# Row vectors that are put in order by two ScalarE copies

## The chip, the cores and the metric

One core of a Trainium2 chip runs the whole program. The time is in microseconds (us) of the device, from the start of the program to its end; three runs of a kernel are given by their median. The engines are named as the profile names them: PE (TensorE matmul; PEld is its weight load), DVE (VectorE), ACT (ScalarE), POOL (GpSimd) and SP (SyncE, which issues the DMAs).

## The reference, cut to what matters

Three transformer layers on 512 tokens of width 1024, in float32. Each sublayer is wrapped in the same two formulas; a third one closes the kernel:

```python
def rms_norm(x, g):
    y = x * rsqrt(mean(x * x, axis=-1) + 1e-6)
    return y * g

mod = silu(c) @ ada_w[layer] + ada_b[layer]            # six vectors of 1024
sh1, sc1, g1, sh2, sc2, g2 = split(mod, 6)
h = rms_norm(x, norm_g[0]) * (1 + sc1) + sh1           # into the sublayer
x = x + g1 * rms_norm(y, norm_g[1])                    # behind it
...
return x + gate * out                                  # last layer
```

So at every border between two sublayers each row of `x` is multiplied elementwise by vectors of 1024 that are the same for every row: `G` (gate times norm gain), `B` (one plus scale, times norm gain) and `S` (shift). In the last layer it is `gate`.

## The kernel before

Everything is recorded as a list of operations first (`Rec.add`), with a cost for each from a formula (`Rec.cost`: for a DVE operation 68 + 1.043 ns per element, for an ACT copy from SBUF 93 + 0.834 ns per element, both whatever the operands' steps). Then a list scheduler (`Rec.order`, `Rec.once`) replays the list on a model of the engines. It picks for each engine the most urgent operation that is ready, gives every tile a slot in a pool of fixed size, and repeats this 12 times with due times worked out from the last pass (`dates`). Of the passes the one with the earliest modelled end is kept. Then each engine gets its operations in that order (`emit`); on the chip every engine follows its own list, and waits where an operand is not there yet. Tiles of up to 2 KB per partition share pool "2", which has 12 slots. A tile may take a slot only while enough are free for all the tiles that come before it in the program and have none yet (`Res.rank`, `place`). A DMA is modelled as landing 650 + 1350 ns and its transfer time (256 KB: 790 ns) after its issue (lines 549 to 551).

A weight GEMM is done in three passes of float32r (high part, and two corrections), so PE has most of the work, and DVE and ACT (now and then POOL) split weights and activations into high and low parts (`wh`, `wl`, `ah`, `al`, in the tail of a GEMM `twh`, `twl`, `tah`, `tal`).

A row vector is first computed with a feature on each partition, a column tile of 128 x 8 (`col`). `wide` (line 953) brings it onto all 128 partitions: one DMA writes the 1024 values to DRAM so that four values of one partition lie side by side, two DMAs read 512 of them each onto all partitions. Thus in the tile the value of feature `128 k + p` of a half stands at `4 p + k`. `wide` returns the tile through a rearranged view, whose innermost step is four elements (16 bytes); the instructions that use it get their other operands through `by4` (line 964), which only names the two axes.

Eleven vectors go through `wide`: `G1, B2, S2` at the end of the first mixer (`gmlp`), `G2` after the first feed-forward layer (its `B` and `S` stay columns, `h_chunk2`), `G3, B4, S4` after the attention (`nsa`), `G5, B6, S6` after the second feed-forward layer, and `gate` at the end of `second`. In the profile the tiles are called `G1w`, `B2w` and so on, and `gatew`. Their users are these:

- `residual` (line 1032), four borders, four chunks of 128 rows, two halves: `z = acc * G` (DVE reads the accumulators in PSUM), then `x = x + r * z`.
- `h_chunk` (line 1002), three borders: `hx = x * B` and then `hx = hx * r + S`, both on DVE or POOL as the scheduler likes; then four PE transposes of `hx` into `tp`, and the split of `tp` into the next layer's `hi` and `lo`.
- `fin` (line 1987): `fy = acc * gate`, then `fy + fx` and the DMA of the result.

`three(rows)` (line 1126) makes the wide tiles; `gmlp` and `nsa` call it ahead of the whole output GEMM, `ff` at `k == 31 - FTAIL`, so eight weight blocks before its end. In `out_gemm` the last `tail` blocks of the contraction are held in SBUF, and the chunks are finished one after the other, so that `done(c, banks)` of a chunk runs while PE does the next chunk.

Of the kernel before, what the change touches and what calls it, by code (L numbers as in the profile page):

```python
# [26 lines left out]
F32 = mybir.dt.float32  # L27
# [645 lines left out]
class KB:  # L673
# [279 lines left out]
    def wide(self, vec, name):  # L953

        v = self.col(vec)
        r = self.scratch([1, 1024], name)
        self.sp.dma_start(r.rearrange("o (n p k) -> p (o n) k", n=2, p=128), v.rearrange("p (n k) -> p n k", n=2))
        t = [self.t2([128, 512], F32, name) for _ in range(2)]
        for n in range(2):
            self.sp.dma_start(t[n], r[:, n * 512:n * 512 + 512].bcast())  # L960
        return [x.rearrange("q (p k) -> q k p", k=4) for x in t]

    @staticmethod
    def by4(x):

        return x.rearrange("q (k p) -> q k p", k=4)


    def x_rstd(self, c, either=False):
# [32 lines left out]
    def h_chunk(self, c, r, B, S, hT, keep=None):  # L1002
        if keep is not None:
            return self.h_chunk2(c, r, B, S, hT, keep)
        for n in range(2):
            s = slice(n * 512, n * 512 + 512)
            t = self.t2([128, 512], F32, "hx")
            self.flex("tensor_mul", self.by4(t), self.by4(self.xs[c][:, s]), B[n])
            self.mac(self.by4(t), self.by4(t), r, S[n])
            ps = self.ps("tp")  # L1010
            for j in range(4):
                self.pe.transpose(ps[:, j * 128:(j + 1) * 128], t[:, j * 128:(j + 1) * 128], self.ident)
            cs = slice(c * 128, c * 128 + 128)
            self.split(hT.hi[n][:, :, cs], hT.lo[n][:, :, cs], ps.rearrange("p (j t) -> p j t", j=4))
# [17 lines left out]
    def residual(self, c, banks, G):  # L1032

        ss = self.st(2, "ys")
        z = []
        for n in range(2):
            s = slice(n * 512, n * 512 + 512)
            junk = self.t2([128, 512], F32, "junk")
            self.act.activation(junk, banks[n], AF.Square, accum_out=ss[:, n:n + 1])
            z.append(self.t2([128, 512], F32, "z"))  # L1040
            self.dve.tensor_mul(self.by4(z[n]), self.by4(banks[n]), G[n])
        r = self.rstd_of(ss, "yr")
        for n in range(2):
            s = slice(n * 512, n * 512 + 512)
            x = self.xs[c][:, s]
            self.mac(x, z[n], r, x)
# [639 lines left out]
    def second(self, hT, grow):  # L1686
# [298 lines left out]
        gate = self.wide(grow, "gatew")  # L1985

        def fin(c, banks):
            for n in range(2):
                s = slice(n * 512, n * 512 + 512)
                xt = self.t2([128, 512], F32, "fx")  # L1990
                self.sp.dma_start(xt, self.xd[c][:, s])
                y = self.t2([128, 512], F32, "fy")
                parts = 2 if c == NC - 1 and n == 1 else 1
                for i in range(parts):
                    h = slice(i * 512 // parts, (i + 1) * 512 // parts)
                    hk = slice(h.start // 128, h.stop // 128)
                    self.dve.tensor_mul(self.by4(y)[:, hk], self.by4(banks[n])[:, hk], gate[n][:, hk])
                    self.dve.tensor_add(y[:, h], y[:, h], xt[:, h])
                    self.sp.dma_start(self.out[0, c * 128:(c + 1) * 128, n * 512 + h.start:n * 512 + h.stop], y[:, h])

        self.out_gemm(self.act_f32(mixed), I["w_out_2"][0], KD, fin, CTAIL, split=True)

    def build(self):
# [87 lines left out]
```

## Time and profile before

| | |
|---|---|
| median of 3 runs | 1549.9 us (1549.61 to 1550.47) |
| the profiled execution | 1551.63 us, its span 1549.6 us |
| PE busy | 1499.1 us (97% of the span) |
| DVE busy | 1128.3 us (73%) |
| ACT busy | 673.0 us (43%) |
| POOL busy | 246.0 us (16%) |

A busy share is an average over the whole span. The span is that of the profiled execution; what a sum from the trace says of it is carried to the median of the runs, which is 1.7 us below the profiled execution's own time. An instruction's name in the profile is `out<-in`. Nearly all instructions carry line 616, that of the recorder, so tiles tell them apart, not lines.

### The profile page before, as it was taken

What the parts mean: (1) busy time and instruction counts of PE and PEld (TensorE: products, weight loads), DVE (VectorE), ACT (ScalarE), POOL (GpSimd) and SP (SyncE); (2) the same over time, 40 slices, a digit from 0 to 9 for tenths busy, and PEclk for the clock granted to TensorE, in tenths of its full rate; (3) what the DMA queues carried; (4) which work ended last, traced back from release to release, by engine and by line L of the source; (5) the groups of instructions that cost most, each with busy time, mean ns of one, the idle gap of its engine ahead of it and who ended that gap; (6) DMA issues with size and microseconds to landing.
All of it is one profiled execution on the core that took longest, in us unless ns stands there. A gap on an engine that the chain in (4) does not pass through costs nothing.

```text
span 1549.6 us, 20206 instructions
## 1 busy us (share of the span) xinstructions
PE 1499.1 (97%) x7426; PEld 1250.1 (81%) x7426; DVE 1128.3 (73%) x2092; ACT 673.0 (43%) x1466; POOL 246.0 (16%) x286
## 2 busy tenths in 40 slices
PE   8998899999999999999999899999999899999988
PEld 6887788888888888778877788888888778878877
DVE  8898975568871779788996964455671778698983
ACT  6533332232120646688893332221120327567770
POOL 1142000000010311343431000000010005122350
PEclk9999999999999999999999999999999999999999
DMA  9863675549620443101014636337311351113112
GB/s 368 278 231 115 220 272 188 169 156 383 268 86 11 138 145 118 51 1 56 29 69 137 206 121 202 112 135 278 129 55 41 102 173 55 55 55 106 31 55 95
DMA packets 117921, 212.96 MB, mean 137 GB/s; under 512 B 16064, under 2 KB 76736, under 8 KB 117824
## 3 DMA queue, kind: packets, MB, share of 16 engines
q1 hardware_dynamic: 117824, 211.69, 39.8%
q8 instruction: 58, 0.95, 0.2%
q14 instruction: 39, 0.32, 0.1%
HBM read 205.33 MB, written 6.34 MB: 137 GB/s over the span
## 4 chain that ended last, share of the span: by engine, by line
PE 70%; DVE 15%; ACT 3%; issue 2%; POOL 1%; POOLq 0%; DVEq 0%; ACTq 0%
PE acc L616 25%; PE fmps L616 24%; PE qps L616 4%; PE tmc L616 3%; DVE hx L616 3%; PE po L616 2%; PE sgps L616 2%; DVE wl L616 2%; DVE ptl L616 2%; DVE z L616 1%; PE kps L616 1%; DVE x L616 1%; PE sB L616 1%; PE vps L616 1%; PE tmb L616 1%
## 5 line engine op out<-in xcount | busy, mean ns | idle before, releaser
L616 DVE TENSOR_TENSOR wl<-raw,wh 128x1024 fp32r<-128x1024 f32 x194 | 240.7, 1243 | 39.4 <-PE fmps L616 18.5
L616 DVE CAST wh<-raw 128x1024 fp32r<-128x1024 f32 x120 | 84.9, 707 | 133.6 <-PE fmps L616 102.0
L616 PE MATMUL acc<-wh,ah 128*128 128x512 f32 x432 | 168.4, 390 | 0.0
L616 PE MATMUL acc<-wl,ah 128*128 128x512 f32 x432 | 168.3, 390 | 0.0
L616 DVE SCALAR_TENSOR_TENSOR raw<-raw,cb 128x1024 f32<-128x1024 f32 x112 | 136.5, 1244 | 0.0
L616 PE MATMUL acc<-wh,al 128*128 128x512 f32 x432 | 133.3, 389 | 0.0
L616 ACT ACTIVATE r<-fmps 128x512 f32<-128x512 f32 x64 | 38.2, 597 | 205.9 <-PE fmps L616 205.9
L616 PE MATMUL fmps<-hfh,wl 128*128 128x512 f32 (+1 forms) x288 | 105.9, 368 | 1.9 <-DVE wl L616 1.9
L616 PE MATMUL acc<-twh,tah 128*128 128x512 f32 x272 | 106.4, 396 | 0.0
L616 PE MATMUL fmps<-hf1h,wl 128*128 128x512 f32 (+1 forms) x288 | 105.4, 366 | 0.8 <-DVE wl L616 0.8
L616 PE MATMUL acc<-twl,tah 128*128 128x512 f32 x272 | 105.8, 395 | 0.0
L616 PE MATMUL fmps<-hfl,wh 128*128 128x512 f32 (+1 forms) x288 | 105.7, 368 | 0.0
L616 PE MATMUL fmps<-hfh,wh 128*128 128x512 f32 (+1 forms) x288 | 105.5, 368 | 0.0
L616 PE MATMUL fmps<-hf1l,wh 128*128 128x512 f32 (+1 forms) x288 | 105.3, 366 | 0.0
L616 PE MATMUL fmps<-hf1h,wh 128*128 128x512 f32 (+1 forms) x288 | 104.9, 366 | 0.0
L616 ACT CAST ah<-hid 128x512 fp32r<-128x512 f32 x48 | 29.8, 620 | 158.9 <-PE acc L616 158.9
L616 PEld LDWEIGHTS acc<-wh,al 128*128 128x128 f32 x432 | 81.1, 188 | 16.8
L616 PEld LDWEIGHTS acc<-wh,ah 128*128 128x128 f32 x432 | 81.2, 188 | 16.7
L616 PEld LDWEIGHTS acc<-wl,ah 128*128 128x128 f32 x432 | 81.1, 188 | 16.6
L616 PE MATMUL acc<-twh,tal 128*128 128x512 f32 x272 | 87.8, 398 | 4.6 <-DVE tal L616 4.6
L616 POOL TENSOR_SCALAR tah<-hid 128x512 fp32r<-128x512 f32 x4 | 3.9, 969 | 476.3 <-DMA raw<-in_ff_w_out_dram 206.3
L616 ACT CAST wh<-raw 128x1024 fp32r<-128x1024 f32 x55 | 57.6, 1049 | 43.0 <-PE fmps L616 30.0
(533 smaller groups left out, 3869.9 us busy)
## 6 DMA issues: line engine op xcount, KB each, us to landing
raw<-in_ada_w_dram SPq DMA_DIRECT2D x40, 1024.0 KB, 7.5
raw<-in_ff_w_in_dram SPq DMA_DIRECT2D x32, 1024.0 KB, 8.8
raw<-in_ff_w_out_dram SPq DMA_DIRECT2D x32, 1024.0 KB, 5.0
raw<-in_w_in_dram SPq DMA_DIRECT2D x16, 1024.0 KB, 5.5
raw<-in_w_ada_dram SPq DMA_DIRECT2D x12, 1024.0 KB, 6.4
raw<-in_ada_w_dram SPq DMA_DIRECT2D x16, 512.0 KB, 9.9
raw<-in_kv_ada_w_dram SPq DMA_DIRECT2D x8, 1024.0 KB, 12.1
raw<-in_a_w_in_dram SPq DMA_DIRECT2D x8, 512.0 KB, 10.2
```

The costliest lines, as they stand in the source:

```text
L616: getattr(real[e], m)(*a, **k)
```

## The change

`wide` allocates two tiles for each half. The DMA reads into the first (`G1wr` and so on, after its name), an ACT copy puts it in order into the second, and the second is returned as it is. `by4` goes; all users read and write plain contiguous tiles. Nothing else is touched: the DMAs, the arithmetic and the scheduler stay.

```diff
@@ wide
-        t = [self.t2([128, 512], F32, name) for _ in range(2)]
+        t = []
         for n in range(2):
-            self.sp.dma_start(t[n], r[:, n * 512:n * 512 + 512].bcast())
-        return [x.rearrange("q (p k) -> q k p", k=4) for x in t]
-
-    @staticmethod
-    def by4(x):
-
-        return x.rearrange("q (k p) -> q k p", k=4)
+            w = self.t2([128, 512], F32, name + "r")
+            self.sp.dma_start(w, r[:, n * 512:n * 512 + 512].bcast())
+            t.append(self.t2([128, 512], F32, name))
+            self.act.copy(t[n].rearrange("q (k p) -> q k p", k=4), w.rearrange("q (p k) -> q k p", k=4))
+        return t
@@ h_chunk
-            self.flex("tensor_mul", self.by4(t), self.by4(self.xs[c][:, s]), B[n])
-            self.mac(self.by4(t), self.by4(t), r, S[n])
+            self.flex("tensor_mul", t, self.xs[c][:, s], B[n])
+            self.mac(t, t, r, S[n])
@@ residual
-            self.dve.tensor_mul(self.by4(z[n]), self.by4(banks[n]), G[n])
+            self.dve.tensor_mul(z[n], banks[n], G[n])
@@ fin
-                    hk = slice(h.start // 128, h.stop // 128)
-                    self.dve.tensor_mul(self.by4(y)[:, hk], self.by4(banks[n])[:, hk], gate[n][:, hk])
+                    self.dve.tensor_mul(y[:, h], banks[n][:, h], gate[n][:, h])
```

## Rows read from the trace of the kernel before

**Rows 1.** The page's first part: busy time of each engine, share, instructions

```profile
PE 1499.1 (97%) x7426; PEld 1250.1 (81%) x7426; DVE 1128.3 (73%) x2092; ACT 673.0 (43%) x1466; POOL 246.0 (16%) x286
```

**Rows 2.** PE's waits, whole span: waiter, releaser, us in total, times, longest

```profile
PE tp L616 <- DVE hx L616: 14.3, 22, 1.7
...
PE acc L616 <- DVE tal L616: 4.6, 2, 3.1
```

**Rows 3.** Groups by form, DVE, vector users: count, busy us, mean ns, idle before

```profile
L616 DVE SCALAR_TENSOR_TENSOR hx<-hx,xr,S2w 128x512 f32<-128x512 f32 x8 | 8.8, 1142 | 0.2
...
L616 DVE TENSOR_TENSOR z<-acc,G3w 128x512 f32<-128x512 f32 x8 | 8.3, 1072 | 11.6 <-PE acc L616 11.6
...
L616 DVE TENSOR_TENSOR hx<-x,B2w 128x512 f32<-128x512 f32 x7 | 7.3, 1084 | 0.0
L616 DVE TENSOR_TENSOR fy<-acc,gatew 128x512 f32<-128x512 f32 x7 | 7.1, 1056 | 21.9 <-PE acc L616 21.9
```

**Rows 4.** Groups by form, DVE: same operations and sizes on other operands

```profile
L616 DVE TENSOR_TENSOR ptl<-tA,pth 128x512 fp32r<-128x512 f32 x36 | 24.7, 687 | 5.8 <-ACT pth L616 5.4
...
L616 DVE SCALAR_TENSOR_TENSOR x<-z,yr,x 128x512 f32<-128x512 f32 x32 | 22.6, 748 | 0.5
...
L616 DVE TENSOR_TENSOR fy<-fy,fx 128x512 f32<-128x512 f32 x7 | 4.6, 691 | 0.0
```

**Rows 5.** PE's waits at the first mixer's border, 140 to 215 us

```profile
PE tp L616 <- DVE hx L616: 2.1, 4, 1.0
PE fmps L616 <- DVE wl L616: 1.9, 1, 1.9
PE tp L616 <- ACT junk L616: 0.7, 1, 0.7
```

**Rows 6.** PE's waits at the attention's border, 835 to 915 us

```profile
PE tp L616 <- DVE hx L616: 5.4, 8, 1.4
PE fmps L616 <- DVE wl L616: 0.8, 1, 0.8
```

**Rows 7.** PE's waits at the second feed-forward layer's border, 1190 to 1270 us

```profile
PE tp L616 <- DVE hx L616: 5.2, 8, 1.7
```

**Rows 8.** PE's waits at the first feed-forward layer's border, 495 to 560 us

```profile
PE tp L616 <- ACT hx L616: 0.6, 1, 0.6
```

**Rows 9.** Timeline, 1242 to 1252 us: start, length, engine, instruction, idle before

```profile
1242.81 1.05 DVE L616 TENSOR_TENSOR z<-acc,G5w 128x512 f32<-128x512 f32 x1
...
1246.75 2.07 DVE L616 TENSOR_TENSOR hx<-x,B6w 128x512 f32<-128x512 f32 x2
...
1246.87 1.06 ACT L616 ACTIVATE junkx<-x 128x1024 f32<-128x1024 f32 x1 [2.47 <-DVE x L616]
...
1248.74 0.15 DVE L616 TENSOR_SCALAR hv<-ss 128x1 f32<-128x1 f32 x1
...
1250.40 2.18 DVE L616 SCALAR_TENSOR_TENSOR hx<-hx,xr,S6w 128x512 f32<-128x512 f32 x2
1251.67 0.63 PE L616 MATMUL tp<-ident,hx 128*128 128x128 f32 x4 [0.99 <-DVE hx L616]
```

**Rows 10.** Busy us of PE, PEld, DVE, ACT, POOL by stretch, PE clock, DMA

```profile
192.00:194.00 2.00, 2.00 (x11) 2.00 (x11) 1.86 (x4) 0.00 (x0) 0.00 (x0) 0.50 1.00 384
194.00:196.00 2.00, 2.00 (x15) 2.00 (x14) 2.00 (x4) 0.80 (x2) 0.00 (x0) 0.71 1.09 350
800.00:825.00 25.00, 21.81 (x123) 15.77 (x122) 24.48 (x66) 22.12 (x59) 9.46 (x14) 1.00 0.34 105
```

**Rows 11.** DMAs of tile `B4w`: time from issue to landing

```profile
DMA to landing us min/median/max: 2.8/5.6/6.0
```

**Rows 12.** Groups by form, ACT: a plain 512-element pass, one with steps of 64 bytes

```profile
L616 ACT ACTIVATE hid<-r 128x512 f32<-128x512 f32 x64 | 40.5, 633 | 2.0
...
L616 ACT ACTIVATE bh<-R,pos 128x124 fp32r<-128x124 f32 x32 | 14.3, 504 | 4.2 <-DVE R L616 4.2
```

**Rows 13.** Timeline, ACT, 820 to 830 us: first split for the attention's output GEMM

```profile
824.77 0.60 ACT L616 CAST ah<-oT 128x512 fp32r<-128x512 f32 x1
```

## The prediction

> **What bounds the kernel now.** I read the shares of the engines first. PE is busy for 1499.1 of 1549.6 us [rows 1], so about 50 us at most can be won without taking work from PE, and a cheaper DVE instruction is worth something only where PE stands still for it. So the second view is the list of PE's waits. Its longest entry is the transposes `tp` that wait for DVE's `hx`: 14.3 us in 22 waits [rows 2]. `hx` is made by the instructions that the change touches. The third view is the same list cut to the four borders. It shows 2.1 + 0.7 + 1.9 us at the first mixer's border [rows 5], 5.4 + 0.8 us at the attention's [rows 6] and 5.2 us at the second feed-forward layer's [rows 7]. (The 0.7 put down to ACT's `junk` is a `tp` like the others; DVE's `hx` ended last there.) At the first feed-forward layer's border there is a wait of 0.6 us for an ACT `hx`, and none for DVE [rows 8]: that border uses only `G2w`, and the change has nothing to win there.
>
> Why DVE is late is in the groups by form. The users of the wide tiles take 1072 ns (`z`), 1084 ns (`hx` product), 1142 ns (`hx` with the shift) and 1056 ns (`fy`) [rows 3]. The same operations of the same size on contiguous operands take 687 ns with a PSUM operand, 691 ns without, and 748 ns for the scalar-tensor-tensor form [rows 4]. The scheduler's own formula gives 68 + 1.043 x 512 = 602 ns to all of them. So its order puts the transposes of a chunk on PE where `hx` would be ready if each of these took 0.6 us, and on the chip each is about half a microsecond later than that.
>
> **Part 1: the users get shorter.** 32 `z` save 1.072 - 0.687 = 0.385 us each, 12.3 us together. 24 `hx` products save 1.084 - 0.691 = 0.393 each, 9.4 us (one of the 24 is on POOL; I count it alike). 24 shifts save 1.142 - 0.748 = 0.394 each, 9.5 us. Eight tiles' worth of `fy` save 1.056 - 0.687 = 0.369 each, 3.0 us. DVE loses about 34 us of work, but only the borders turn that into time.
>
> What of it lies on PE's path is read from one chunk [rows 9]. The chain is `z` twice, `rstd`, `x`, then two `hx` products while ACT squares `x` (`junkx`), the statistics `hv`, the shift, the transposes. The two products take 2.07 us, ACT's square 1.06 us, and `hv` starts at 1248.74, when the products are done: DVE ends this leg, not ACT. With 0.69 each the products end 0.7 us earlier, about with ACT's square and its short accumulator read, so nearly all of that gain stays. One `z` of the two is surely on the chain (0.385), the first shift too (0.394). The chain gets shorter by 0.385 + 0.7 + 0.394 = 1.5 us, up to 1.9 with both `z`. The longest wait in each list is 1.0, 1.4 and 1.7 us [rows 5 to 7]; a chain that is 1.5 us shorter removes all but some tenths. What stays is the short second wait of a chunk, about 0.2 us, of which I keep half (12 chunks, 1.2 us in all). So of 2.1 + 0.7 + 5.4 + 5.2 = 13.4 us I take 12.2.
>
> The two waits of `fmps` for a `wl` (1.9 and 0.8 us) come right behind a border, when DVE's list is behind: DVE is busy for 1.86 and 2.00 of 2 us there [rows 10]. A chunk takes 2 x (0.385 + 0.393 + 0.394) = 2.3 us off that list, so both go: 2.7 us. Behind the 1.9 us wait PE's granted clock is 0.50 and 0.71 of full speed in two stretches of 2 us [rows 10], so 1.2 GHz for most of that time; before it PE had stood idle. That costs 2 x 0.50 + 2 x 0.29 = 1.6 us. Whether it goes with the wait the trace can't say; I take half, 0.8, with 0 and 1.6 as ends. At the end of the kernel the last two `fy` products of 256 elements save about 0.3 us together (half of two times 0.369, estimated from [rows 3, 4]). The sum of the gain is 12.2 + 2.7 + 0.8 + 0.3 = 16.0 us; its upper end is 13.4 + 2.7 + 1.6 + 0.3 = 18.0.
>
> **Part 2: 22 copies on ACT.** No copy with this step is in the trace. A plain pass of 512 elements from SBUF takes 633 ns [rows 12]: the lower end. A pass of 124 elements in steps of 64 bytes takes 504 ns [rows 12]; scaled by length that is 504 x 512 / 124 = 2.08 us, the upper end. I take 633 + 385 = 1.02 us, the surcharge that the same tiles cost DVE. The 22 copies then are 22.4 us (13.9 to 45.8) on an engine that is busy for 43% of the span [rows 1].
>
> The Trainium skill, "SBUF — State Buffer", section "Specifications (TRN2)", speaks against the change at this point: SBUF has lines of 16 bytes, at least two hits per line are needed for full bandwidth, and each crossing to a new line costs. A step of four floats crosses at every element, so by this rule the penalty isn't removed: it moves to the copies, once per tile instead of once per use. It agrees with 1072 against 687 ns, and no run shows it for ACT. By the rule a copy has the surcharge, and the sum stands as it is made here; without one (633 ns) the cost term of 5.0 below would be 3.1, and the time 1537.
>
> **Part 3: a new wait on ACT, and more slots.** The copy waits for a DMA on ACT's list. The scheduler's model has the DMA land 2.8 us after issue; the rows have 2.8 to 6.0 [rows 11]. So a copy can hold ACT for up to 3.2 us, and what is queued behind it waits too. The lists differ:
>
> - After the feed-forward layers (`G2w`; `G5w`, `B6w`, `S6w`) ACT has little to do, the operand splits run some blocks ahead of PE, and the wide tiles are read while PE still has the whole tail of the GEMM to do. I cost these eight copies at nothing; if the splits had no lead, a copy would cost its 1.02 us.
> - At the first mixer (`G1w`, `B2w`) `tah` and, behind it, DVE's `tal` are queued on the copies, and PE waits for `tal` already, 4.6 us in two waits [rows 2]. 0 to 5.2 us for each vector (3.2 and two copies). `S2w` lands about when the first chunk's statistics start; its copies can hold `junk` for 1 to 2 us, which that chunk's shorter chain pays back. I take 1.5 us for the stage.
> - At the attention's end (`G3w`, `B4w`, `S4w`) ACT is busy for 22.12 of 25 us [rows 10], with the splits that feed PE. Six copies are 6.1 us there. In pool "2" the three vectors now need 12 tiles in the program's order, all 12 slots, ahead of the first `ah` of the output GEMM, which ran at 824.77 [rows 13] and fills PE's gaps from then on. 0 to 15.6 us (three times 5.2); I take half of the copies, 3.0.
> - `gatew`: ACT is full there too, but the tile is used only behind the output GEMM, and the due times can hold the copy back. 0 to 5.2; I take 0.5.
>
> Sum of the costs: 5.0 us, the ends 0 and 31 (six vectors, 5.2 each).
>
> **Part 4: the new order.** The scheduler sees 22 more operations and 22 more tiles, and keeps the best of 12 passes of a heuristic. Its costs for the users are unchanged, so nothing pulls the borders apart. But all behind the first mixer may be put in another order, and some 30 us of PE's idle time lies outside the borders. I count this as 0, with 3 us to either side.
>
> **The sum.** The profiled execution: 1551.6 - 16.0 + 5.0 = 1540.6 us, of it 2.0 around the span. The median of the runs lies 1.7 us lower: 1549.9 - 11 = 1539 us.
>
> **The rivals.**
>
> - ACT's leg takes over. ACT's `junk` and `junkx`, and weight splits between the short steps, bind the chain once DVE is quick, and only one `z` and the shift count: 0.78 us in each of 12 chunks, 9.4 us, some 8.3 as waits below that can't give it (estimated), and half of the `wl` waits, 1.3. Less the same 5.0: 1549.9 - 4.6 = 1545. For it: a `wl` of 1.2 us stands between `hv` and the shift in the chunk I read. Against: `hv` there waited for DVE.
> - Slower: the copies hold ACT at the attention's end and the first mixer, where PE lives from ACT's splits. Place and price are those of Part 3, up to 31 us; it decides the sign once more than 16 us of that reach PE. With 21 us it gives 1555. For it: ACT is at 88% there, landings are late by up to 3.2 us, and the slots are just used up. Against: 16 us need nearly all the stalls to be on PE's path, and the due times put the copies behind urgent splits.
> - The new order eats the gain: another pass is kept, with waits elsewhere that cancel the borders' gain. 1550, give or take 3. For it: 12 passes of a heuristic; against: it would have to lose 11 us that it didn't lose before.
> - The users don't get shorter. Then only the costs stay, 1550 to 1555. Two rows with the step and three without, same operations, speak against it; it shares the chance of the slower case.
>
> **Chances.** Forecast 0.62, with an own range of 1532 to 1544. ACT's leg 0.18. New order 0.11. Slower 0.09. A measurement of this kernel can tell about 0.2% (3.1 us) from no change. Faster by more than that: 0.62, 0.13 of the second, a little of the third, 0.76. Same: 0.12. Slower: 0.12, of the third 0.03. The range goes from 1532 (the upper gain of 18.0 at no cost) to 1549, just within no change; it leaves out some 0.15 above and 0.05 below.
>
> **What would show it.** Right: `z`, both `hx` and `fy` at 0.69 to 0.75 us in the groups by form; the entry `tp` for `hx` down from 14.3 to below 3 us; no 1.9 us wait for `wl` and no fall of the clock near 192 us; 22 copies of 0.63 to 1.02 us on ACT. Wrong: new PE waits at 115 to 135 or 800 to 832 us for `tal`, `pth` or `ah`, ACT idle for a DMA ahead of a copy, or `tp` waits that stay with `hv` released by ACT.

## The result, and the profile after

The changed kernel takes 1529.0 us (median of 4 runs, 1527.1 to 1529.8); the kernel before took 1549.8 us beside it (4 runs, 1548.5 to 1550.5). The ratio is 0.9865, with an interval of 0.9848 to 0.9882. That is 20.8 us less, where 11 were forecast; the time lies 3 us below the range. The profiled execution of the changed kernel took 1529.35 us, 1527.0 of it in the span.

First the page of the changed kernel: busy time of each engine.

```profile
PE 1494.3 (98%) x7426; PEld 1249.5 (82%) x7426; DVE 1092.5 (72%) x2090; ACT 696.0 (46%) x1489; POOL 247.6 (16%) x287
```

Against [rows 1] DVE is busy for 35.8 us less and ACT for 23.0 more. PE executes the same 7426 matmuls and yet is busy for 4.8 us less; for that the forecast has only the 0.8 us of its clock term. PE's idle time, span less busy, falls from 50.5 to 32.7 us.

The users of the vectors and three of the copies, in the groups by form of the changed kernel (busy us, mean ns of one, idle time before them):

```profile
L616 DVE SCALAR_TENSOR_TENSOR hx<-hx,xr,S2w 128x512 f32<-128x512 f32 x8 | 5.6, 747 | 0.2
...
L616 DVE TENSOR_TENSOR z<-acc,G3w 128x512 f32<-128x512 f32 x8 | 5.2, 685 | 13.0 <-PE acc L616 13.0
...
L616 DVE TENSOR_TENSOR fy<-acc,gatew 128x512 f32<-128x512 f32 x7 | 4.6, 687 | 23.7 <-PE acc L616 23.7
L616 DVE TENSOR_TENSOR hx<-x,B2w 128x512 f32<-128x512 f32 x7 | 4.5, 684 | 0.0
...
L616 ACT COPY G5w<-G5wr 128x512 f32<-128x512 f32 x2 | 2.2, 1122 | 6.3 <-DMA G5wr<-G5w 6.3
...
L616 ACT COPY B4w<-B4wr 128x512 f32<-128x512 f32 x2 | 2.2, 1177 | 0.0
...
L616 ACT COPY S6w<-S6wr 128x512 f32<-128x512 f32 x2 | 2.2, 1096 | 3.3 <-DMA S6wr<-S6w 3.2
```

The users have the lengths of their contiguous twins [rows 4] to a few nanoseconds. A copy takes 1.10 to 1.18 us. Where the last column names a DMA, ACT stood still ahead of its copies: 6.3 us for the two of `G5w`, nothing for `B4w` at the attention's end.

PE's waits in the changed kernel (in all, times, longest): the head of the list of the whole span, then the whole list of 1160 to 1275 us, where the second feed-forward layer's border now lies. From 835 to 915 us, the attention's border, the list is empty.

```profile
PE dot L616 <- POOL do L616: 2.7, 4, 0.9
PE po L616 <- ACT pth L616: 2.5, 4, 0.9
PE fmps L616 <- DVE hv L616: 2.0, 1, 2.0
PE acc L616 <- DVE tal L616: 2.0, 2, 1.4
PE vps L616 <- ACT hh L616: 2.0, 1, 2.0
PE tp L616 <- DVE hx L616: 2.0, 3, 0.8
```

```profile
PE po L616 <- DVE pth L616: 0.2, 1, 0.2
```

The `tp` entry fell from 14.3 us in 22 waits [rows 2] to 2.0 in 3. The wait at the end of the first mixer's border did not go: `fmps` stood still for 1.9 us there, put down to `wl` [rows 5], and does so for 2.0 us now, put down to `hv`, in front of the same product of `hfh` and `wl`. The timeline of one chunk of the second feed-forward layer's border shows how the `tp` waits went (start, length, engine, instruction, idle before); it is the counterpart of [rows 9]:

```profile
1222.98 0.69 DVE L616 TENSOR_TENSOR z<-acc,G5w 128x512 f32<-128x512 f32 x1 [0.19 <-ACT junk L616]
...
1226.57 1.28 DVE L616 TENSOR_TENSOR hx<-x,B6w 128x512 f32<-128x512 f32 x2
1226.68 1.06 ACT L616 ACTIVATE junkx<-x 128x1024 f32<-128x1024 f32 x1 [2.47 <-DVE x L616]
...
1227.86 0.15 DVE L616 TENSOR_SCALAR hv<-ss 128x1 f32<-128x1 f32 x1
...
1229.54 1.41 DVE L616 SCALAR_TENSOR_TENSOR hx<-hx,xr,S6w 128x512 f32<-128x512 f32 x2
...
1230.97 0.60 PE L616 MATMUL tp<-ident,hx 128*128 128x128 f32 x4
```

The two products take 1.28 us instead of 2.07 and end at 1227.85, just as ACT's square is done; `hv` follows at once. The two shifts take 1.41 instead of 2.18, and `tp` has no wait in front of it.

To see where the time went I cut the span at instructions that every kernel has: the first matmul `pm`, the first `z` (the first user of a wide tile), and the matmuls with the last `fmps<-hfh,wh`, the last `qps<-hbh,wh`, the last `fmps<-hf1h,wh` and the first `kps`. In the trace of before they start at 110.5, 147.5, 359.2, 761.6, 1057.6 and 1264.6 us. This table is worked out from those starts; it gives the us that each profiled execution saves against that of before.

```
                           to 111  111-z  z-359  359-762   762-1058  1058-1265  1265-end   span
holds                              ahead  mixer,            attn end, 2nd ff     output
                                   of z   border  1st ff    border    border
changed kernel               0.9    4.0    3.9     0.5        5.1       6.7       1.5     22.6
e1  no copies                1.6    2.8    6.7     0.6        7.8       6.7      -1.5     24.7
e3  step of 2, no copies     0.8    2.0    6.8     0.7        7.8       6.7      -1.3     23.5
e4  step of 8, no copies     0.3    2.8   -1.2    -0.3       -1.2      -2.7      -0.2     -2.5
e8  changed, plain copies    0.4    3.9    5.9     0.4        6.9       6.7       1.8     26.0
e9  changed, write in steps  1.4    3.9    4.2     0.5        6.4       6.7       1.8     24.9
e6  only z and fy short      1.1    2.1    2.1     0.7        3.1       3.0       0.2     12.3
e7  only hx short            0.8    2.0    5.3     0.0        5.7       5.9      -1.3     18.4
e2  plain copies alone       1.4    4.0    0.6    -0.5       -1.0       0.0       1.2      5.7
e5  scattered write          1.0   -9.0    4.8     0.7        6.3       6.7      -1.2      9.3
e10 copies on POOL          -1.0    1.7    2.3     1.3       -4.8       6.7      -3.1      3.1
```

No changed instruction runs ahead of 111 us, so the first column (-1.0 to 1.6) shows about how far two executions differ by themselves. In e10 the order is another one from 64 us on.

### The profile page after: what moved, and what is told of

Read it like the earlier page. It is cut to its first block, busy times and chain, and to the rows that moved or that the text cites. A ratio compares the mean times of both kernels' runs of the same rounds, so it can differ in the third digit from the quotient of the medians.

```text
span 1527.0 us, 20220 instructions
## 1 busy us (share of the span) xinstructions
PE 1494.3 (98%) x7426; PEld 1249.5 (82%) x7426; DVE 1092.5 (72%) x2090; ACT 696.0 (46%) x1489; POOL 247.6 (16%) x287
## 4 chain that ended last, share of the span: by engine, by line
PE 76%; DVE 6%; ACT 4%; issue 1%; POOL 1%; POOLq 0%; DVEq 0%; ACTq 0%
PE acc L616 28%; PE fmps L616 25%; PE qps L616 4%; PE tmc L616 3%; PE po L616 3%; PE sgps L616 2%; PE tmb L616 1%; DVE ptl L616 1%; PE kps L616 1%; PE sB L616 1%; DVE wl L616 1%; PE sA L616 1%; PE vps L616 1%; PE tp L616 1%; PE tA L616 1%
## 5 line engine op out<-in xcount | busy, mean ns | idle before, releaser
L616 PEld LDWEIGHTS acc<-wh,ah 128*128 128x128 f32 x432 | 81.5, 189 | 16.9
L616 PEld LDWEIGHTS acc<-wl,ah 128*128 128x128 f32 x432 | 81.2, 188 | 16.8
L616 PEld LDWEIGHTS acc<-wh,al 128*128 128x128 f32 x432 | 81.1, 188 | 16.8
```

The lines of the kernel that those rows point to most:

```text
L616: getattr(real[e], m)(*a, **k)
```

## The experiments

**e1: the gain alone.** No copies; the users read the tiles as the DMA wrote them.

```
-            w = self.t2([128, 512], F32, name + "r")
-            self.sp.dma_start(w, r[:, n * 512:n * 512 + 512].bcast())
-            t.append(self.t2([128, 512], F32, name))
-            self.act.copy(t[n].rearrange("q (k p) -> q k p", k=4), w.rearrange("q (p k) -> q k p", k=4))
+            self.sp.dma_start(t[n], r[:, n * 512:n * 512 + 512].bcast())
```

> The users read contiguous tiles, and there is no copy: the wide tiles keep the order in which the DMA lays them down, so the vectors are permuted, and all instructions stand in the order of the kernel before. Theory A (the step in the users is the gain, whatever the order): about 1529 us, as the changed kernel. Theory B (two parts, the users' step at the borders, and the new order of the changed kernel, above all its first mixer's tail): the borders' waits of PE for hx and wl go, 14 to 16 us, while the 4.6 us of waits for tal and the fall of the clock at 130 to 140 us stay: 1534 to 1537 us. Theory C (the new order is nearly all): 1546 to 1550.

1527.3 us (1525.4 to 1528.3), ratio 0.9848 [0.9834, 0.9861]: by the ratio 23.6 us less than before, with the instructions of every engine in the order of before. So the short users give such a gain by themselves, and no new order is needed for it. The 1534 to 1537 us, which went by the listed idle time and let the waits for `tal` and the clock behind them stay, are missed by some 8 us. The page of e1:

```profile
PE 1491.2 (98%) x7426; PEld 1247.3 (82%) x7426; DVE 1094.6 (72%) x2092; ACT 673.0 (44%) x1466; POOL 245.3 (16%) x286
```

PE's idle time is 1524.9 - 1491.2 = 33.7 us, 16.8 less than before, and that part is about what the forecast had. The other 7.9 us are busy time of PE. The rows of before show two things that it holds, the end of a matmul and the clock. PE's timeline just ahead of a wait (the row after the last of these is the `tp` of [rows 9]):

```profile
1249.62 0.39 PE L616 MATMUL tmb<-wh,h2l 128*128 128x512 f32 x1
1249.84 0.39 PE L616 MATMUL tmb<-wh,h2h 128*128 128x512 f32 x1
1250.07 0.39 PE L616 MATMUL tmb<-wl,h2h 128*128 128x512 f32 x1
1250.30 0.39 PE L616 MATMUL tmb<-wh,h2l 128*128 128x512 f32 x1
```

A matmul is recorded for 0.39 us, but the next one starts 0.227 us behind it. Without a wait `tp` would have started at 1250.30 + 0.23 = 1250.53; it started at 1251.67. PE lost 1.14 us, and the row lists 0.99: the end of the last matmul, 0.15 us beyond the start of a next one (its drain), is counted as busy. This can be tried on the borders. At the attention's, 5.4 + 0.8 us in 9 waits [rows 6] and 9 x 0.15 give 7.6; e1 and e3, which have no wait left there, save 7.8. At the second feed-forward layer's, 5.2 us in 8 waits [rows 7] and 8 x 0.15 give 6.4; all seven kernels with all users short save 6.7.

The clock has to be taken apart by place. In the trace of before, PE around a wait for `tal`, busy time with the clock (PE, PEld, DVE, ACT, POOL, then PE's clock), and the first user of a wide tile:

```profile
131.19 1.22 PE L616 MATMUL acc<-twh,tal 128*128 128x512 f32 x2 [3.14 <-DVE tal L616]
...
137.26 0.39 PE L616 MATMUL acc<-twh,tah 128*128 128x512 f32 x1
```

```profile
130.00:140.00 10.00, 8.80 (x26) 7.02 (x27) 10.00 (x13) 1.67 (x2) 0.59 (x1) 0.66 0.17 71
```

```profile
147.46 2.04 DVE L616 TENSOR_TENSOR z<-acc,G1w 128x512 f32<-128x512 f32 x2 [3.94 <-PE acc L616]
```

The granted clock is 0.66 from 130 to 140 us, and PE starts again at 131.19. The 14 matmuls from there to 137.26 take 6.07 us, where 14 x 0.227 are 3.18: 2.9 us are lost. But all this lies ahead of the first `z`, and there before and e1 run the same instructions in the same order. In e3 the wait is as long, and the clock does not fall:

```profile
PE acc L616 <- DVE tal L616: 4.3, 2, 3.1
```

```profile
130.00:140.00 10.00, 9.22 (x39) 7.17 (x40) 10.00 (x15) 1.67 (x2) 0.00 (x1) 1.00 0.14 57
```

From 111 us to the first `z`, e1 wins 2.8 us and e3, e6 and e7 2.0 or 2.1, but e4, whose users are slower than those of before, wins 2.8 as well. So this part isn't the users' work, and why before is late there stays open.

Behind the first `z` before has one fall of the clock, 1.6 us at 192 us [rows 10], and e1 has none there. At this border the listed waits fall from 4.9 us in 7 ([rows 5] and 0.2 us for `yr`) to one of 0.5. These 4.4 us, six drains of 0.15 and the 1.6 us are 6.9; the stretch from the first `z` to 359 us saved 6.7. At the three borders together e1 saves 6.7 + 7.8 + 6.7 = 21.2 us, and e3 21.3. That much is tied to the short users place by place. With the 0.6 us from 359 to 762 us it is 21.8 in e1; the 23.6 us of the ratio have an interval of 21.5 to 25.7.

**e2: copies and order alone.** The kernel before with plain copies, the users still stepping; the order of the instructions is that of the changed kernel.

```
-        t = [self.t2([128, 512], F32, name) for _ in range(2)]
+        t = []
         for n in range(2):
-            self.sp.dma_start(t[n], r[:, n * 512:n * 512 + 512].bcast())
+            w = self.t2([128, 512], F32, name + "r")
+            self.sp.dma_start(w, r[:, n * 512:n * 512 + 512].bcast())
+            t.append(self.t2([128, 512], F32, name))
+            self.act.copy(t[n], w)
```

> The 22 copies on ACT are there, but plain and contiguous (0.63 us each), and the users still read with a step of four elements, so all instructions stand in the order of the changed kernel. Theory A: no gain, 1550 to 1553 us. Theory B: the waits for tal at the first mixer's tail are 2 us instead of 4.6 and the clock doesn't fall there, 6 us, while the borders' waits stay: 1542 to 1545 us. Theory C: about 1530.

1547.5 us (1546.1 to 1550.3), ratio 0.9979 [0.9970, 0.9988]: 3.3 us less than before, in spite of 22 copies of 0.62 us. The entry for `tp` stays; in the list of waits of e2:

```profile
PE tp L616 <- DVE hx L616: 15.0, 21, 1.7
...
PE acc L616 <- DVE tal L616: 2.0, 2, 1.4
```

What it wins lies for the most part ahead of the first `z` (4.0), where the new order has waits for `tal` of 2.0 us instead of 4.6 and no fall of the clock at 130 to 140 us. Kernels in the order of before win 2.0 to 2.8 there too, so only 1 or 2 us of the 4.0 are the order's. At the attention's end it loses 1.0. So the new order is worth a few microseconds at most by itself, and most of the gain isn't due to it.

**e3 and e4: other steps.** The kernel before, with a step of 2 and of 8 elements in place of 4.

```
-        return [x.rearrange("q (p k) -> q k p", k=4) for x in t]
+        return [x.rearrange("q (p k) -> q k p", k=2) for x in t]      (e4: k=8; the same in by4)
```

> The kernel before with a step of two elements (8 bytes) in the users in place of four; the vectors are permuted, the order of the instructions is that of the kernel before. If a line of 16 bytes decides, two hits fall into each line and z takes its contiguous 0.69 us, the shift 0.75. If each step costs, z stays at 1.07. If the cost grows with the distance, about 0.85.

> The kernel before with a step of eight elements (32 bytes); the vectors are permuted, the order of the instructions is that of the kernel before. If a line of 16 bytes decides, one hit per line as with four elements: z at 1.07 us. If the cost grows with the distance, z at 1.4 us or more.

One execution each: 1528.2 us with 2, 1554.1 us with 8. One group of e3, then two of e4:

```profile
L616 DVE TENSOR_TENSOR z<-acc,G3w 128x512 f32<-128x512 f32 x8 | 5.2, 685 | 12.3 <-PE acc L616 12.3
```

```profile
L616 DVE TENSOR_TENSOR hx<-x,B4w 128x512 f32<-128x512 f32 x8 | 8.8, 1148 | 0.0
L616 DVE TENSOR_TENSOR z<-acc,G3w 128x512 f32<-128x512 f32 x8 | 8.8, 1131 | 11.6 <-PE acc L616 11.6
```

A step of 8 bytes costs nothing, one of 16 bytes 0.385 us for 512 elements [rows 3, 4], one of 32 bytes 0.45. The penalty isn't for stepping as such, and twice the distance adds little to it. With step 2 the kernel has the time of e1 in the order of before, a second way to the same gain.

**e5: the order made by the DMA.** The write to DRAM puts single elements in place, and no copies are needed; PE, DVE, ACT and POOL keep the order of before.

```
-        self.sp.dma_start(r.rearrange("o (n p k) -> p (o n) k", n=2, p=128), v.rearrange("p (n k) -> p n k", n=2))
+        self.sp.dma_start(r.rearrange("o (n k p) -> p (o n) k", n=2, p=128), v.rearrange("p (n k) -> p n k", n=2))
```

> The DMA that writes a vector to DRAM puts each of its 1024 elements in its final place, one element at a time, so the tiles arrive in order: no copy on ACT, the users contiguous, the instructions in the order of the kernel before. If the users' step is the gain and ACT's copies cost what the difference between the run without copies and the changed kernel shows (some 2 us), this gives 1526 to 1528 us, a little below the changed kernel. If the scattered write is slow (1024 pieces of 4 bytes), it lands later; at the first mixer and the attention's end a vector could then come late, and PE waits for z: 1530 or more.

1539.0 us (1537.7 to 1542.4), ratio 0.9929 [0.9916, 0.9942]. SP's timeline in the kernel before, then in e5, and then PE's longest wait in e5 and the clock around that:

```profile
111.75 0.37 SPq L616 DMA_DIRECT2D G1w<-G  x1
...
114.58 0.81 SPq L616 DMA_DIRECT2D G1w<-G1w  x2
```

```profile
110.73 0.37 SPq L616 DMA_DIRECT2D G1w<-G  x1
112.45 0.42 SPq L616 DMA_DIRECT2D B2w<-B  x1
122.92 0.90 SPq L616 DMA_DIRECT2D G1w<-G1w  x2
134.38 0.80 SPq L616 DMA_DIRECT2D B2w<-B2w  x2
```

```profile
PE acc L616 <- ACT twh L616: 8.5, 1, 8.5
```

```profile
140.00:150.00 10.00, 6.49 (x17) 5.01 (x18) 6.51 (x9) 3.13 (x4) 3.36 (x2) 0.55 0.33 133
```

The read of `G1w` is issued 12.2 us after its write; in the kernel before it was 2.8. SP's list stands behind it, the weights for `twh` come late, PE waits for 8.5 us and then has half its clock for some microseconds. Both later borders keep most of their gain or all of it (6.3, 6.7); ahead of the first `z` 9.0 us are lost. So at the first mixer the vectors' way through DRAM has no room for a slower write, and a copy on ACT is the cheaper place to put them in order.

**e6 and e7: which users count.** Only `z` and `fy` contiguous, or only the two `hx` steps; no copies, the order of before.

> Order of the kernel before, no copies, G and gate contiguous (z and fy at 0.69 us), B and S with the step of four (both hx at 1.08 and 1.14); the vectors G are permuted, and so is gate. If both z of a chunk are on PE's path (0.77 us per chunk), the first wait of most chunks falls below half: 9 to 11 us, 1540 to 1542. If only one is (0.385): 4 to 6 us, 1545 to 1547.

> Order of the kernel before, no copies, B and S contiguous (hx at 0.69 and 0.75 us), G and gate with the step of four (z and fy at 1.07); the vectors B and S are permuted. The two products and the first shift take 0.7 + 0.39 = 1.1 us off a chunk's chain, and the second wait of each chunk goes: 14 to 18 us, 1533 to 1537. If ACT's square of x takes over from the products, only the shift counts: 6 to 8 us, 1543 to 1545.

e6: 1539.8 us, ratio 0.9936 [0.9922, 0.9949]. e7: 1533.4 us, ratio 0.9891 [0.9875, 0.9906]. The `tp` entry of e6, then of e7:

```profile
PE tp L616 <- DVE hx L616: 8.4, 18, 1.0
```

```profile
PE tp L616 <- DVE hx L616: 2.7, 5, 0.8
```

By the ratios the one saves 9.9 us and the other 16.9; together 26.8, where e1 with both saves 23.6. Both lie on the chain, the `hx` steps with more of it, as the forecast had it (0.385 against 0.7 + 0.394 a chunk). At the second feed-forward layer's border, where the clock is full, e6 saves 3.0 us in four chunks: about both `z` of a chunk (0.77 us), where the forecast counted one as sure. The 3 us that the sum has over e1 would fit a common part (once a wait is gone, a shorter chain gives nothing more), but they lie within the intervals and show nothing by themselves.

**e8 and e9: what the copies' step costs.** The changed kernel with plain copies, and with copies that read in order and write with the step. Both have the order of the changed kernel.

```
-            self.act.copy(t[n].rearrange("q (k p) -> q k p", k=4), w.rearrange("q (p k) -> q k p", k=4))
+            self.act.copy(t[n], w)                                                                        (e8)
+            self.act.copy(t[n].rearrange("q (k p) -> q p k", k=4), w.rearrange("q (p k) -> q p k", k=4))  (e9)
```

> The changed kernel, same order of all instructions, users contiguous, but the 22 copies plain (0.63 us instead of 1.13); the vectors are permuted. It takes 11 us off ACT. If the length of the copies reaches PE at the attention's end, as I costed, half of 6 x 0.5 us goes: 1 to 3 us below the changed kernel, 1526 to 1528. If only the wait for the DMAs and the new order count there, no change: 1529.

> The changed kernel with one edit: the 22 ACT copies read their source in order and write with the step of 16 bytes, where the changed kernel reads with the step and writes in order. They move the same numbers to the same places, and the order of the instructions on every engine is that of the changed kernel. Theory 1: only a read with the step costs more. Then a copy takes about 0.62 us as the plain copies did, and the kernel comes to the time of the run with plain copies, 1525 to 1526 us. Theory 2: a write with the step costs as much as a read. Then a copy takes 1.10 to 1.18 us and the time is that of the changed kernel, 1528 to 1530 us.

e8: 1525.5 us (1525.0 to 1525.9), ratio 0.9837 [0.9824, 0.9851]. e9: 1527.3 us (1525.5 to 1530.3), ratio 0.9851 [0.9838, 0.9864]. One group of e8, then one of e9:

```profile
L616 ACT COPY B4w<-B4wr 128x512 f32<-128x512 f32 x2 | 1.2, 643 | 0.0
```

```profile
L616 ACT COPY B4w<-B4wr 128x512 f32<-128x512 f32 x2 | 2.1, 1179 | 0.0
```

A write with the step costs ACT as much as a read, 1.11 to 1.18 us against 0.61 to 0.64: on this point the second expectation of e9 is right. The times do not follow as neatly. By the ratios the step costs the changed kernel 4.3 us and e9 2.2, with copies of the same length, and the intervals touch or overlap. The clock shows why a difference of this size can't be given to the copies. PE stands still for 2.0 us at about 180 us in all three kernels, in e8 with the name that the forecast used:

```profile
PE fmps L616 <- DVE wl L616: 2.0, 1, 2.0
```

These are stretches behind that wait, of the changed kernel and then of e8:

```profile
182.00:184.00 2.00, 2.00 (x14) 2.00 (x15) 1.86 (x6) 0.41 (x2) 0.00 (x0) 0.84 1.08 384
184.00:186.00 2.00, 2.00 (x12) 2.00 (x11) 1.59 (x3) 0.40 (x1) 0.00 (x0) 0.50 1.02 387
186.00:188.00 2.00, 2.00 (x15) 2.00 (x15) 1.20 (x2) 0.77 (x2) 0.00 (x0) 0.81 1.12 358
```

```profile
182.00:184.00 2.00, 2.00 (x17) 2.00 (x18) 1.86 (x5) 0.41 (x2) 0.00 (x0) 1.00 1.07 380
184.00:186.00 2.00, 2.00 (x20) 2.00 (x18) 2.00 (x4) 1.18 (x2) 0.00 (x0) 1.00 1.03 391
```

The changed kernel loses 2 x (0.16 + 0.50 + 0.19) = 1.7 us to the clock here, e9 as much (0.53 and 0.61 from 182 to 186 us), and e8 nothing. Another 1.7 us of the changed kernel go at 810 to 830 us (clock 0.91 and 0.92), in neither of the others. The four executions of the changed kernel have mean clocks of 0.995 to 0.999, and the one with 0.999 has the shortest span, 1524.8 us. So the step of the copies costs between nothing and about 4 us; how much of it is the copies' own length stays open.

**e10: the copies on POOL.** The changed kernel with a multiplication by one on POOL; the scheduler makes another order of the whole program.

```
-            self.act.copy(t[n].rearrange("q (k p) -> q k p", k=4), w.rearrange("q (p k) -> q k p", k=4))
+            self.pcopy(t[n].rearrange("q (k p) -> q k p", k=4), w.rearrange("q (p k) -> q k p", k=4))
```

> The changed kernel with the 22 copies on POOL (a multiplication by one) instead of ACT; the scheduler puts the whole program in another order for it. Theory 1: the copies cost time because ACT is full at the attention's end; POOL, busy for 16% of the span, can take them for nothing, and the kernel comes near the run without copies, 1524 to 1528 us, with POOL's copies at 0.6 to 1.2 us each. Theory 2: what costs is the waiting for the late DMA and the slots, whichever engine copies, or POOL's copies are 1.5 us or longer: then 1529 to 1533 us, with PE waits for a tile that POOL or its wait holds back. As the order is another one, a difference below 2 us says nothing for either.

1550.1 us (1547.5 to 1554.1, 11 runs), ratio 0.9999 [0.9990, 1.0008]: all of the gain is lost, far more than either expectation. POOL's timeline at the attention's end, PE's longest wait, and the clock:

```profile
826.71 3.04 POOL L616 TENSOR_SCALAR G3w<-G3wr 128x512 f32<-128x512 f32 x1
829.72 1.10 POOL L616 TENSOR_SCALAR B4w<-B4wr 128x512 f32<-128x512 f32 x1
830.78 1.59 POOL L616 TENSOR_SCALAR ah<-oT 128x512 fp32r<-128x512 f32 x1
```

```profile
PE acc L616 <- POOL ah L616: 3.5, 1, 3.5
```

```profile
830.00:840.00 10.00, 7.58 (x24) 6.39 (x25) 6.36 (x8) 1.97 (x4) 5.60 (x5) 0.66 0.78 219
```

A copy on POOL takes 1.1 to 3.0 us. The split `ah` stands behind the copies on POOL's list, and PE waits 3.5 us for it. From its next start at 832.4 to 838 us it has half its clock, which costs about 2.8 us. This is the forecast's slower rival, on another engine. It isn't all of the loss: the mean clock of all e10's executions is 0.984 to 0.990, against 0.995 to 0.999 in the changed kernel, and against the changed kernel it is behind at the first mixer, at the attention's end and after 1265 us. The order as a whole is worse; which of its parts costs what wasn't taken apart.

## Why the prediction was right in its direction and too small

- **What bounds the kernel, and where the change acts: right.** e1 has the gain without copies and without a new order, and 21.2 of the 24.7 us of its profiled execution lie at the three borders that the waits named. The first feed-forward layer's border gave nothing, as forecast (0.4 to 0.7 us from 359 to 762 us in six of the seven kernels with all users short, 1.3 in e10).
- **Part 1, lengths and `tp`: right.** `z`, both `hx` and `fy` are as long as their twins. `hv` starts when the products and ACT's square end together. The `tp` waits fell by 12.3 us, with 12.2 taken. (The scheduler's formula adds 61 ns for the shift, so 663 and not 602; no sum uses it.)
- **Part 1, the two waits of `fmps`: half right.** That of 0.8 us at the attention's border is gone. That of 1.9 us at the first mixer's is down to 0.5 in the order of before (e1), but stays at 2.0 in the order of the changed kernel, in e8 and e9 too, and the clock fell behind it in the changed kernel and in e9. The sum took it as gone; why the new order keeps it was not taken apart.
- **Part 1, the size: the step that failed.** The sum of 16.0 us took the listed idle time as the price of a stall, and 18.0 as its upper end. For the three borders it had 15.7 (16.0 without the end of the kernel); e1 and e3 save 21.2 and 21.3 there. The term that was left out is the drain: 24 waits at the borders at 0.15 us are 3.6. Two more were too small: the second waits of the chunks go whole, not by half (1.2 more), and with the wait at 190 us all of its clock comes back (0.8 more; it may come back but need not, as e4 has a wait of 2.1 us there without a fall). Together 15.7 + 3.6 + 1.2 + 0.8 = 21.3. With the drain alone the upper end would have been 21.6, and the range would have reached 1528. The deeper fall of the clock at 130 to 140 us was rightly left out: it lies ahead of all users.
- **Part 2, the copies' length: near.** 1.10 to 1.18 us against 1.02; the surcharge on ACT is about 0.50 us where DVE's is 0.385. By the rule of the Trainium skill, "SBUF — State Buffer", section "Specifications (TRN2)", a step that meets each 16-byte line only once is slow. The runs agree beyond what the rows of before could show: two elements per line cost nothing (e3), one per line costs on DVE and on ACT, reading (the changed kernel) and writing (e9). The penalty did move to the copies.
- **Part 3, the costs: not settled.** The changed kernel is slower than e1 by 0.0017 of 1550, 2.6 us, where 5.0 were taken. The intervals of the two ratios overlap, so the cost could be near nothing. In the profiled executions it is 1.6 us from 111 to 359 us (1.5 taken) and 2.7 at the attention's end (3.0 taken), and the last stretch gives 3.0 back, which the forecast did not have. That these come so near is in part luck: each of the first two holds 1.7 us of a fall of the clock in the changed kernel, and the third one of e1 (0.83 from 1480 to 1490 us). ACT did stand still for DMAs ahead of copies behind the feed-forward layers, 17.6 us in all for `G2w`, `G5w`, `B6w` and `S6w`, and it cost PE nothing: the lead of the splits was there. At the attention's end no copy waited for its DMA.
- **Part 4, the order: taken as 0 with 3 to either side.** e2 puts it at 3.3 us of gain, net of its plain copies and with what before loses ahead of the first `z`, so the value taken was low and the bound about right for this order. e10 shows that the bound is far too narrow for an order in general.
- **The rivals.** ACT's leg did not take over: no `tp` wait at the two later borders is left. The slower one did not happen on ACT; in e10 its wait did happen, on POOL. The users did get shorter.

By the ratios both errors point the same way: 23.6 - 16.0 = 7.6 us from the gain and 5.0 - 2.6 = 2.4 us from the cost make the 10 us by which the time was missed. Of the 7.6, the borders show 5.5 (21.2 less 15.7); the rest and the 2.4 lie within the intervals.

## What to carry to other kernels

A stall of PE costs more than its idle row: add the drain of the matmul in front of it (recorded length less the distance to the next one, here 0.15 us each), and look through the windows for a fall of the clock behind every wait that the edit removes or shortens. When the result is there, cut the span at the first instruction that the edit changes: what differs ahead of it, waits and clock, is not the edit's gain. Where a strided read is used several times, order the tile once on an engine with slack, but not behind work that the bounding engine waits for. Where a scheduler makes the order, the same edit on another engine can cost the whole gain, so a change is judged with its order, and its mechanism apart from it, with the order held fixed.

## What the runs showed of the hardware that was not expected

- A step of two float32 elements is free on DVE (685 ns for 512), one of four costs 0.385 us and one of eight 0.45.
- On ACT a step of four elements costs 0.50 us for 512, on the reading or on the writing side alike.
- A DMA that writes 1024 single elements of 4 bytes holds its reader back for 12.2 us, where 256 pieces of 16 bytes took 2.8 (`G1w`).
- The granted clock falls behind some waits of 2 us and not behind others: at the same place, with a wait of the same length, 0.50 in the changed kernel and 1.00 in e8. Behind one of 3.1 us it is 0.50 in before and 1.00 in e3.
